# One 8 KB tile in place of two 4 KB ones for streamed expert weights, and router logits on four column tiles, in a two-layer decoder trunk

## The chip, the cores and the metric

The kernel runs on one core of a Trainium2 chip. The metric is the device time of one execution in microseconds (us). The engines are named as in the profile: PE is TensorE (PEld its weight loads), DVE is VectorE, ACT is ScalarE, POOL is GpSimd, SP is SyncE, whose queue issues nearly all DMAs here. A "tile" of weights below is 128 partitions x 2048 f32, which is 1 MB (1,048,576 bytes).

## The reference

256 tokens of 1024 channels go through two layers. Layer 0 is a mixer (attention beside a recurrent block) and a dense SwiGLU. Layer 1 is a pooling mixer and a mixture of 8 experts, two for each token. Cut to layer 1, which the change mostly touches:

```python
def rms_norm(x, g, eps=NORM_EPS):
    xf = x.astype(jnp.float32)
    y = xf * lax.rsqrt(jnp.mean(xf * xf, axis=-1, keepdims=True) + eps)
    return (y * g.astype(jnp.float32)).astype(x.dtype)
...
def pool_mixer(h, pool_w, pool_scale):
...
    for g, w in enumerate(POOL_WINDOWS):          # 4 groups of channels, windows 2, 4, 8, 16
...
        outs.append((cs - lower) / count - xg)    # mean over the window, minus the token itself
    d = jnp.stack(outs, axis=2).astype(h.dtype)
    y = jnp.einsum("bsgc,gcd->bsgd", d, pool_w).reshape(bsz, seq, D_MODEL)
    return y * pool_scale
...
def moe_swiglu(h, router_w, wg, wu, wd):
    t = h.reshape(-1, dm)
    logits = (t @ router_w).astype(jnp.float32)           # 256 x 8
    top_val, top_idx = lax.top_k(logits, TOP_K)           # 2 of 8
    gates = jax.nn.softmax(top_val, axis=-1)
    combine = jnp.sum(jax.nn.one_hot(top_idx, N_EXPERTS) * gates[..., None], axis=1)
    for e in range(N_EXPERTS):
        he = jax.nn.silu(t @ wg[e]) * (t @ wu[e])         # 1024 -> 3584
        out = out + (combine[:, e:e + 1] * he) @ wd[e]    # 3584 -> 1024
...
            h = h + pool_mixer(rms_norm(h, ln_mix_odd[j]), pool_w[j], pool_scale[j])
            h = h + moe_swiglu(rms_norm(h, ln_ffn_odd[j]), router_w[j], moe_wg[j], moe_wu[j], moe_wd[j])
    return rms_norm(h, final_g)
```

## The kernel before

**Streams and slots.** All weights are listed once, in the order of use (`order`), as 1 MB tiles: layer 0, one for the pooling mixer, then the experts' (`m_gu`, `m_dn`: 8 experts x 7 steps x 6 tiles = 336). `load_to` takes the next tile of the list, takes the next slot of the list `slots`, and issues the DMA on SP's queue; a slot is an SBUF buffer that is used again when the tile in it has been used. SP is strictly in order, and the DMAs go through eight completion semaphores in turn (`DMAHW0` to `DMAHW7` in the waits below), so that a DMA is issued only after the one eight places before it has landed. `load_free` issues as many loads as there are free slots. The number of slots grows as the program frees memory: `more_slots` puts a buffer at the head of the list; by the experts' stage there are 22.

**Splits.** Up to the pooling mixer the weights are used as pairs of fp32r numbers: `split_half` takes half a tile, ACT writes its rounded part (`hi`) and DVE or POOL the rest (`lo`). Both come from the pool `halves`, tags `hi` and `lo`, five buffers of 4 KB a partition each. When the splits run out, these buffers become slots of the experts' stream: the class `Two` takes one `hi` and one `lo` buffer, and a 1 MB tile is loaded into them by two DMAs of 512 KB, whose rows are 4 KB a partition (`twohi`, `twolo`). There are five such slots among the 22; the other 17 are 8 KB a partition and take one DMA of 1 MB.

**From the dense layer to the experts** the work is one chain. The last `down` piece of the dense layer is added to `h`; PE transposes `h`; ACT and DVE write its halves `xph`, `xpl` (`halve_pair`, four pairs); `rs` (1/rms of each token) comes from the sums of squares `ssq` by nine small DVE steps (`rs_steps`); PE multiplies with the pooling weights (`pw`); ACT and DVE scale the result with `rs` and halve it (`hh`, `hl`); PE applies the windows (`pd`); DVE adds to `h`; PE transposes again and ACT and DVE copy to `hT`. Then the router: `logits` multiplies `hT` with `rw` (16 products with 8 columns, two PE instructions each), `finish_rs` makes the new `rs`, DVE ranks the logits (`ahead`, `rank`, `mskb`), PE counts positions (`pos`), and DVE writes the selection `selr`, which holds `rs`. PE gathers the first expert's tokens with it (`xe`). `keep_warm` issues bf16 products that nobody reads.

**The experts' stage** runs 56 steps. In each, `gate_up_main` multiplies the tokens with four tiles of `m_gu` (`mg`), `gate_up_more` does the same for tokens beyond 64 where an expert has them (`go`), and `down_main`, `down_more` use two tiles of `m_dn` (`y`, `yo`). A step's four `m_gu` slots are given back when its last `mg` product has been issued (`finished`).

## Time and profile before

| | |
|---|---|
| time, median of 3 runs | 1165.93 us (1165.09 to 1167.14) |
| the profiled execution's own time | 1164.08 us |
| its span in the profile | 1162.2 us |
| PE, DVE, ACT, POOL busy | 96%, 26%, 21%, 7% of the span |
| DMA engines' share, mean rate | 87.7%, 352 GB/s |
| read from HBM | 406.62 MB |

"Busy" is a mean over stages with different limits, and a busy PE is not PE at its peak. DMA share is how much of the time the 16 DMA engines moved packets; slightly over 1 means that packets overlap.

### The profile page before, as it was taken

The numbers are of one execution on the slowest core, as the hardware profiler recorded it, in microseconds if no ns is written. First come the engines' busy times: TensorE is split into PE (matmuls) and PEld (weight loads), VectorE is DVE, ScalarE is ACT, GpSimd is POOL, SyncE is SP. The second block draws the span as 40 slices with busy tenths as digits, with TensorE's granted clock in tenths as the row PEclk, the third lists the DMA queues.
The fourth block names the chain that finished last, engine by engine and source line by source line (L and its number), as shares of the span: only waits on it lengthen the run. The fifth ranks groups of instructions, "written<-read, shape, count | busy, mean of one in ns | idle before, by whom it ended". The sixth has DMA issues, their size and how long they took to land.

```text
span 1162.2 us, 16786 instructions
## 1 busy us (share of the span) xinstructions
PE 1116.7 (96%) x7033; PEld 575.3 (50%) x7033; DVE 303.2 (26%) x592; ACT 248.3 (21%) x499; POOL 87.1 (7%) x110
## 2 busy tenths in 40 slices
PE   8999999999999999988989999999999999999995
PEld 7777999999843333322323343333334433433331
DVE  6686565454721111110101110111110011011112
ACT  5865544444510010010001000100000010001012
POOL 1613151121200000000000000000000000000000
PEclk9999999999999999999999999999999999999998
DMA  9434955555999999999999999999999999999991
GB/s 357 159 136 174 364 195 184 186 178 183 331 366 417 418 415 419 416 417 419 414 421 413 420 414 417 418 400 421 415 418 406 417 419 415 420 387 420 415 414 64
DMA packets 69910, 409.19 MB, mean 352 GB/s; under 512 B 7856, under 2 KB 8112, under 8 KB 31536
## 3 DMA queue, kind: packets, MB, share of 16 engines
q1 hardware_dynamic: 69664, 407.60, 87.7%
q8 instruction: 80, 1.31, 0.5%
q10 hardware_dynamic: 144, 0.10, 0.0%
q14 instruction: 22, 0.18, 0.0%
HBM read 406.62 MB, written 1.05 MB: 351 GB/s over the span
## 4 chain that ended last, share of the span: by engine, by line
PE 69%; DMA 22%; DVE 4%; ACT 3%; issue 1%; SPq 0%; DVEq 0%; ACTq 0%
PE mg L970 24%; PE y L1016 11%; PE gu L185 11%; DMA raw<-in_m_gu 8%; PE go L981 6%; PE dn L185 5%; PE yo L1026 3%; DMA raw<-in_m_dn 3%; PE xe L952 2%; DMA spare<-in_m_gu 2%; PE tp L1005 2%; DMA spare<-in_m_dn 1%; DMA twolo<-in_m_gu 1%; DMA twohi<-in_m_gu 1%; DMA sparehl<-in_m_gu 1%; PE wo L185 1%
## 5 line engine op out<-in xcount | busy, mean ns | idle before, releaser
L970 PE MATMUL mg<-raw,xe 128*64 128x512 f32 x928 | 219.9, 601 | 11.6 <-DMA raw<-in_m_gu 11.3
L999 DVE TENSOR_TENSOR sg<-sg,mg 128x256 f32<-128x256 f32 x56 | 23.6, 421 | 581.9 <-ACT sg L998 581.9
L998 ACT ACTIVATE sg<-mg 128x256 f32<-128x256 f32 x56 | 21.5, 383 | 560.4 <-PE mg L970 560.4
L168 DVE TENSOR_TENSOR lo<-raw,hi 128x1024 fp32r<-128x1024 f32 x84 | 106.3, 1285 | 97.9 <-ACT hi L167 97.6
L970 PEld LDWEIGHTS mg<-raw,xe 128*64 128x64 f32 x928 | 59.4, 136 | 126.6 <-issue 92.6
L167 ACT ACTIVATE hi<-raw 128x1024 fp32r<-128x1024 f32 x96 | 98.7, 1051 | 43.6 <-PE dn L185 25.0
L1016 PE MATMUL y<-raw,het 128*64 128x512 f32 x432 | 99.3, 594 | 1.1 <-DMA raw<-in_m_dn 1.0
L1007 ACT COPY het<-tp 128x384 f32<-128x384 f32 x56 | 26.7, 477 | 169.3 <-PE tp L1005 169.3
L1016 PEld LDWEIGHTS y<-raw,het 128*64 128x64 f32 x432 | 30.6, 137 | 64.6 <-issue 56.4
L970 PE MATMUL mg<-twolo,xe 128*64 128x512 f32 x212 | 55.5, 602 | 0.6 <-DMA twolo<-in_m_gu 0.6
L970 PE MATMUL mg<-twohi,xe 128*64 128x512 f32 x212 | 55.3, 604 | 0.7 <-DMA twohi<-in_m_gu 0.7
L1016 PE MATMUL y<-twohi,het 128*64 128x512 f32 x120 | 54.8, 593 | 0.5 <-ACT het L1007 0.5
L1016 PE MATMUL y<-twolo,het 128*64 128x512 f32 x120 | 54.7, 593 | 0.2 <-DMA twolo<-in_m_dn 0.2
L185 PE MATMUL gu<-xfl,hi 128*128 128x256 f32 x352 | 50.3, 283 | 0.0
L185 PE MATMUL gu<-xfh,hi 128*128 128x256 f32 x352 | 50.1, 283 | 0.0
L185 PE MATMUL gu<-xfh,lo 128*128 128x256 f32 x352 | 50.1, 283 | 0.0
L185 PEld LDWEIGHTS gu<-xfh,hi 128*128 128x128 f32 x352 | 46.2, 191 | 0.9
L185 PEld LDWEIGHTS gu<-xfl,hi 128*128 128x128 f32 x352 | 45.7, 192 | 0.2 <-DVE xfl L270 0.2
L185 PEld LDWEIGHTS gu<-xfh,lo 128*128 128x128 f32 x352 | 45.7, 192 | 0.0
L970 PE MATMUL mg<-spare,xe 128*64 128x512 f32 x168 | 41.3, 602 | 3.1 <-DMA spare<-in_m_gu 3.1
L981 PE MATMUL go<-raw,xe 128*32 128x256 f32 x704 | 41.8, 380 | 0.0
L1005 PEld LDWEIGHTS tp<-pr,sg 128*128 128x128 f32 x168 | 17.4, 141 | 46.4 <-issue 44.6
(380 smaller groups left out, 1372.9 us busy)
## 6 DMA issues: line engine op xcount, KB each, us to landing
raw<-in_m_gu SPq DMA_DIRECT2D x116, 1024.0 KB, 18.6
raw<-in_m_dn SPq DMA_DIRECT2D x54, 1024.0 KB, 19.0
twohi<-in_m_gu SPq DMA_DIRECT2D x53, 512.0 KB, 13.8
twolo<-in_m_gu SPq DMA_DIRECT2D x53, 512.0 KB, 12.6
raw<-in_w_gu SPq DMA_DIRECT2D x22, 1024.0 KB, 5.0
spare<-in_m_gu SPq DMA_DIRECT2D x21, 1024.0 KB, 15.9
twohi<-in_m_dn SPq DMA_DIRECT2D x30, 512.0 KB, 13.8
...
```

Source lines behind the costliest of these rows:

```text
L167: act.activation(hi, r, AF.Copy)
L168: eng.tensor_tensor(lo, r, hi.bitcast(F32), op=OP.subtract)
L185: pe.matmul(dst, l, r, start=start, stop=stop)
L952: pe.matmul(v_[:, k], h[:, t, (4 * k4 + k) * P:(4 * k4 + k + 1) * P], s_[:, t, :], start=t == 0, stop=t == NT - 1)
L970: pe.matmul(b[c * C0:(c + 1) * C0], x_[:, k, 0:C0], block(MOE[n] + k // 2, (k % 2 * 2 + c) * 512), start=k == 0, stop=k == 1)
L981: pe.matmul(go[q:q + C1, 0:2 * P], x_[:, k, C0:CAP], block(MOE[n] + k // 2, (k % 2 * 2 + c) * 512 + r * 2 * P, 2 * P), start=k == 0, stop= ...
L998: act.activation(v_, g_[:, :, 0, :], AF.Silu)
L999: dve.tensor_tensor(v_, v_, g_[:, :, 1, :], op=OP.mult)
L1005: pe.transpose(b[:, i * P:(i + 1) * P], sg[:, i, :], ident)
L1007: act.copy(het[n].rearrange("p a c -> p (a c)"), b[:, 0:3 * P])
L1016: pe.matmul(y_[e][j * C0:(j + 1) * C0], het[n][:, r, c * C0:(c + 1) * C0], block(DOWN[n] + c, (2 * j + r) * 512), start=p == c == r == 0, ...
L1026: pe.matmul(yo[q:q + C1], het[n][:, 2, (2 * c + r) * C1:(2 * c + r + 1) * C1], block(DOWN[n] + c, (2 * j + r) * 512), start=p == r == 0, s ...
```

## The change

It does three things. (1) `hi` and `lo` of a half tile become the two halves of one tile (`hl`, tag `two`, 8 KB a partition, five buffers), so a slot made of one takes one DMA of 1 MB, like the others. (2) `rw` is padded with zeros from 8 to 32 columns, and the logits are made transposed: `rw` is the stationary side, four products with 256 moving columns run on four column tiles of PE, twice; DVE copies the four partial sums (`lp`), PE transposes them back, DVE adds them up in two reductions. (3) For the second `rs`, DVE does the first two steps and POOL the other ten; they stand ahead of the reductions in the program. Beside that, in the pooling mixer all four pairs are halved before the steps to the first `rs`, where these steps stood between the pairs; `selr` takes `rw`'s buffer; two `keep_warm` counts go from 8 to 12 and from 4 to 5. The load of `rw` now writes 8 pieces of 32 bytes a partition, and waits for POOL's memset of `rw`.

```diff
-WARM = (8, 4, 8)
+WARM = (12, 5, 8)
...
-    class Two:
-
-        def __init__(self):
-            self.t = [halves.tile([P, W // 2], F32, tag=t_, name="two" + t_) for t_ in ("hi", "lo")]
...
+    def two():
+
+        return Again(halves.tile([P, W], F32, tag="two", name="two"))
...
-            cut = 2 if i < 2 or isinstance(r, list) else 4 if i == len(order) - 1 else 1
+            cut = 2 if i < 2 else 4 if i == len(order) - 1 else 1
...
-                sp.dma_start(r[a] if isinstance(r, list) else r[:, s_], order[i][1][:, s_])
+                sp.dma_start(r[:, s_], order[i][1][:, s_])
...
-        hi, lo = split[i, a] = [halves.tile([P, W // 2], F32R, tag=tag, name=f"{tag}{i}{a}") for tag in ("hi", "lo")]
+        both = halves.tile([P, W], F32R, tag="two", name=f"hl{i}{a}")
+        hi, lo = split[i, a] = [both[:, u * W // 2:(u + 1) * W // 2] for u in range(2)]
...
+    def finish_rs_pool(part):
+        v_, t_, w_ = nwt[:, 0, 0:NT], nwt[:, 1, 0:NT], nwt[:, 1, 4:4 + NT]
+        if part == 0:
+            dve.scalar_tensor_tensor(v_, ssq[:, :, 0], 1e-6, ssq[:, :, 1], op0=OP.add, op1=OP.add)
+            dve.tensor_scalar(rs.bitcast(I32), v_.bitcast(I32), -0.5, float(0x5F1FFFF9), op0=OP.mult, op1=OP.add)
+            return
+        pool.tensor_tensor(t_, rs, rs, op=OP.mult)
...
+        pool.tensor_tensor(rs, rs, t_, op=OP.mult)
...
-    rw = late.tile([P, KD, E], F32, name="rw")
+    rw = late.tile([P, KD, C1], F32, name="rw")
...
-        sp.dma_start(rw, rtr)
+        pool.memset(rw, 0.0)
+        sp.dma_start(rw[:, :, 0:E], rtr)
...
-    more_slots([Two(), Two()])
+    more_slots([two(), two()])
...
+    for kk in range(2, 4):
+        halve_pair(kk, tb[kk], xp, lno)
     squares(1, (1,))
-    halve_pair(2, tb[2], xp, lno, steps)
-    for step in steps:
-        step()
+    finish_rs()
...
-    run_piece(pool_products, {0: [F(halve_pair, 3, tb[3], xp, lno)], 1.5: [F(mixed_out, 0, 0)],
+    run_piece(pool_products, {1.5: [F(mixed_out, 0, 0)],
...
-    def logits(b):
-        for t in range(NT):
-            for k in range(KD):
-                pe.matmul(b[:, t * E:(t + 1) * E], hT[:, k, t * P:(t + 1) * P], rw[:, k, :], start=k == 0, stop=k == KD - 1)
+    def logits():
+
+        b = bank("tp", "lg")
+        for k2 in range(2):
+            for q in range(4):
+                pe.matmul(b[q * C1:(q + 1) * C1, 0:S], rw[:, 4 * k2 + q, :], hT[:, 4 * k2 + q, :], start=k2 == 0, stop=k2 == 1)
+        squares(1)
+        lp = keep.tile([P, S], F32, tag="row", name="lp")
+        dve.tensor_copy(lp, b[:, 0:S])
+        b = bank("gu", "lt")
+        for t in range(NT):
+            pe.transpose(b[:, t * P:(t + 1) * P], lp[:, t * P:(t + 1) * P], ident)
+        keep_warm(WARM[0], ones)
+        finish_rs_pool(0)
+        for t in range(NT):
+            dve.tensor_reduce(lg[:, t], b[:, t * P:(t + 1) * P].rearrange("p (q e) -> p e q", q=4)[:, 0:E, :], axis=AX.X, op=OP.add)
...
-    squares(1)
-    finish_rs()
-    lgb = bank("tp", "lg")
-    logits(lgb)
+    logits()
+    finish_rs_pool(1)
...
-    keep_warm(WARM[0], ones)
-
-    dve.tensor_copy(lg, lgb[:, 0:NT * E].rearrange("p (t e) -> p t e", t=NT))
```

Where instructions move, in the order of the program. SP's queue before, at the point where the slots of the splits join the experts' stream (`raw`, `spare` are slots of one 1 MB tile; `DMAHW` numbers are the eight completion semaphores):

```order
L144 DMA raw_3051<-in_m_dn 128x2048 [waits DMAHW4_49,DVE_49]
L144 DMA twohi<-in_m_gu 128x1024 [waits DMAHW5_49,PE_49]
L144 DMA twolo<-in_m_gu 128x1024 [waits DMAHW6_49,PE_49]
L144 DMA raw_3100<-in_m_gu 128x2048 [waits DMAHW7_49,DVE_49]
L144 DMA twohi<-in_m_gu 128x1024 [waits DMAHW0_49,PE_49]
L144 DMA twolo<-in_m_gu 128x1024 [waits DMAHW1_49,PE_49]
L144 DMA twohi<-in_m_gu 128x1024 [waits DMAHW2_49,PE_49]
L144 DMA twolo<-in_m_gu 128x1024 [waits DMAHW3_49,PE_49]
L144 DMA twohi<-in_m_dn 128x1024 [waits DMAHW4_49,PE_49]
L144 DMA twolo<-in_m_dn 128x1024 [waits DMAHW5_49]
```

The same place of the changed kernel:

```order
L140 DMA raw_2958<-in_m_dn 128x2048 [waits DMAHW4_49,DVE_49]
L140 DMA two<-in_m_gu 128x2048 [waits DMAHW5_49,PE_49]
L140 DMA raw_3003<-in_m_gu 128x2048 [waits DMAHW6_49,DVE_49]
L140 DMA two<-in_m_gu 128x2048 [waits DMAHW7_49,PE_49]
L140 DMA two<-in_m_gu 128x2048 [waits DMAHW0_49,PE_49]
L140 DMA two<-in_m_dn 128x2048 [waits DMAHW1_49,PE_49]
```

Each pair of 512 KB DMAs is one of 1 MB; which tile goes to which slot stays the same. PE before, from the last transposes of `h` to the first `keep_warm`:

```order
L258 MATMUL xt_3327<-pr,h 128x128 x3
L836 MATMUL lg<-rw,hT 128x8 [waits DMAHW2_49]
L836 MATMUL lg<-rw,hT 128x8
L836 MATMUL lg<-rw,hT 128x8 [waits DVE_49]
L836 MATMUL lg<-rw,hT 128x8
L836 MATMUL lg<-rw,hT 128x8 [waits Activation_49]
L836 MATMUL lg<-rw,hT 128x8
L836 MATMUL lg<-rw,hT 128x8 [waits DVE_49]
L836 MATMUL lg<-rw,hT 128x8 x9
L89 LDWEIGHTS cs
```

and in the changed kernel:

```order
L272 MATMUL xt_3222<-pr,h 128x128 x3
L852 MATMUL lg<-hT,rw 32x256 [waits DMAHW2_49]
L852 MATMUL lg<-hT,rw 32x256
L852 MATMUL lg<-hT,rw 32x256 [waits DVE_49]
L852 MATMUL lg<-hT,rw 32x256
L852 MATMUL lg<-hT,rw 32x256 [waits Activation_49]
L852 MATMUL lg<-hT,rw 32x256
L852 MATMUL lg<-hT,rw 32x256 [waits DVE_49]
L852 MATMUL lg<-hT,rw 32x256
L858 MATMUL lt<-pr,lp 128x128 [waits DVE_49]
L858 MATMUL lt<-pr,lp 128x128
L89 LDWEIGHTS cs
```

Sixteen products became eight, and a pair of transposes that waits for DVE's copy stands behind them. DVE of the changed kernel from the last copy to `hT` to the selection (`rt__1111` holds the logits, then the ranks):

```order
L882 COPY hT<-xt_3222 128x512 [waits PE_49]
L855 COPY lp<-lg 128x256 [waits PE_49]
L249 SCALAR_TENSOR_TENSOR nwt<-ssq 128x2 [waits Activation_49]
L250 TENSOR_SCALAR rs<-nwt 128x2 [waits DVE_49]
L862 TENSOR_REDUCE rt__1111<-lt 128x8 [waits PE_49]
L862 TENSOR_REDUCE rt__1111<-lt 128x8
L889 TENSOR_TENSOR ahead<-rt__1111 128x16x8 [waits DVE_49]
...
L959 TENSOR_SCALAR selr<-cs,rt__1111,rs 128x96 [waits DVE_49,Pool_49]
```

and POOL of the changed kernel, which before has nothing between the scaling of the pooling weights and the end:

```order
L252 TENSOR_TENSOR nwt<-rs 128x2 [waits DVE_49]
L253 TENSOR_TENSOR nwt<-nwt 128x2 [waits Pool_49]
L254 TENSOR_SCALAR nwt<-nwt 128x2 [waits Pool_49]
...
L260 TENSOR_SCALAR nwt<-nwt 128x2 [waits Pool_49]
L261 TENSOR_TENSOR rs<-rs,nwt 128x2 [waits Pool_49]
```

Of the nine `rs` steps that DVE had ahead of the copy of the logits, two are left there; the other ten are a chain on POOL, each waiting for the one before, and `selr` now waits for POOL too.

## Rows read from the trace of the kernel before

**Rows 1.** Busy time by stretch of the span (us from its start): length, then busy us and instructions of PE, PEld, DVE, ACT, POOL; granted clock of PE; DMA share; GB/s.

```profile
337.00:480.00 143.00, 142.17 (x691) 51.72 (x693) 19.31 (x50) 13.45 (x38) 0.00 (x0) 1.00 1.01 414
480.00:608.70 128.70, 112.71 (x506) 34.88 (x502) 13.55 (x34) 10.43 (x29) 0.00 (x0) 1.00 1.02 418
608.70:784.00 175.30, 175.30 (x1225) 66.14 (x1227) 21.54 (x53) 14.19 (x39) 0.00 (x0) 1.00 1.01 414
784.00:822.00 38.00, 33.37 (x161) 11.12 (x155) 3.08 (x7) 2.54 (x7) 0.00 (x0) 1.00 1.01 419
822.00:1143.00 321.00, 320.91 (x2298) 120.48 (x2298) 35.33 (x86) 24.73 (x69) 0.00 (x0) 1.00 0.99 403
```

**Rows 2.** The chain of work that ended last, in order of time: start, length, what.

```profile
588.75 19.88 DMA raw<-in_m_gu
...
802.05 19.88 DMA raw<-in_m_gu
...
821.98 1.94 PE mg L970 x8
```

**Rows 3.** SP's queue, issues in order of time: start, length, engine, line, what.

```profile
322.84 0.33 SPq L144 DMA_DIRECT2D spare<-in_m_dn  x1
335.91 2.57 SPq L144 DMA_DIRECT2D raw<-in_m_gu  x4
```

**Rows 4.** Stretches of 2 us, columns as in rows 1.

```profile
324.00:326.00 2.00, 1.94 (x14) 1.13 (x12) 1.22 (x7) 0.46 (x2) 0.00 (x0) 0.50 1.00 418
...
334.00:336.00 2.00, 2.00 (x13) 0.60 (x11) 0.00 (x0) 0.00 (x0) 0.00 (x0) 1.00 0.21 82
336.00:338.00 2.00, 1.06 (x6) 0.18 (x4) 0.62 (x2) 0.55 (x2) 0.00 (x0) 1.00 0.56 115
```

**Rows 5.** Stretches in which nearly all bytes moved in 4 KB packets (`twohi`, `twolo`), columns as in rows 1.

```profile
370.20:377.20 7.00, 7.00 (x41) 3.43 (x39) 0.56 (x1) 0.48 (x1) 0.00 (x0) 1.00 1.02 409
420.40:427.40 7.00, 7.00 (x35) 2.46 (x34) 2.04 (x3) 1.05 (x2) 0.00 (x0) 1.00 1.03 410
...
522.00:527.40 5.40, 4.99 (x24) 1.66 (x24) 0.87 (x2) 0.48 (x1) 0.00 (x0) 1.00 1.02 406
```

**Rows 6.** Stretches in which all data moved in 8 KB packets (the other slots).

```profile
381.00:412.00 31.00, 31.00 (x155) 11.61 (x153) 3.70 (x9) 3.09 (x9) 0.00 (x0) 1.00 1.01 420
...
533.00:562.00 29.00, 24.48 (x112) 8.08 (x114) 3.30 (x11) 2.06 (x6) 0.00 (x0) 1.00 1.01 421
```

**Rows 7.** DMA packets of 337 to 822 us, and below of 337 to 609 us.

```profile
DMA packets 34243, 201.48 MB, mean 415 GB/s; under 512 B 3793, under 2 KB 3793, under 8 KB 15583
...
DMA packets 19098, 113.12 MB, mean 416 GB/s; under 512 B 2112, under 2 KB 2112, under 8 KB 8512
```

**Rows 8.** DVE in order of time: start, length, line, what, shapes, count, and in brackets the idle time ahead of it and what ended that. Where a count is over 1, the length is that of all together.

```profile
309.10 0.48 DVE L270 SCALAR_TENSOR_TENSOR xpl<-xt,pr,xph 128x256 fp32r<-128x256 f32 x1 [0.41 <-ACT xph L268]
...
311.41 0.88 DVE L270 SCALAR_TENSOR_TENSOR xpl<-xt,pr,xph 128x256 fp32r<-128x256 f32 x2
312.30 2.07 DVE L216 SCALAR_TENSOR_TENSOR hl<-pw,rs,hh 128x512 fp32r<-128x512 f32 x3
...
319.33 0.69 DVE L856 COPY hT<-xt 128x512 f32<-128x512 f32 x1 [0.21 <-PE xt L258]
320.88 0.16 DVE L243 SCALAR_TENSOR_TENSOR nwt<-ssq 128x2 f32<-128x2 f32 x1 [0.86 <-ACT junk L239]
321.07 0.17 DVE L223 TENSOR_SCALAR rs<-nwt 128x2 int32<-128x2 int32 x1
...
323.01 0.29 DVE L867 TENSOR_TENSOR ahead<-rt__1143 128x128 bf16<-128x128 f32 x1
...
324.87 0.57 DVE L937 TENSOR_SCALAR selr<-cs,rt__1143,rs 128x96 f32<-128x96 f32 x2
```

**Rows 9.** PE in order of time, columns as in rows 8.

```profile
311.36 0.40 PE L185 MATMUL pw<-lo,xph 128*128 128x256 f32 x2
311.95 0.78 PE L185 MATMUL pw<-hi,xpl 128*128 128x256 f32 x2 [0.20 <-DVE xpl L270]
...
314.00 0.28 PE L817 MATMUL pd<-hh,ba 128*128 128x256 f32 x1
...
319.13 3.64 PE L836 MATMUL lg<-rw,hT 128*128 128x8 f32 x32
...
325.56 4.06 PE L952 MATMUL xe<-selr,h 128*128 128x96 f32 x32
```

**Rows 10.** Pieces of PE in the chain that ended last: products on four column tiles (32 products, 64 instructions), and a later gather.

```profile
660.30 3.59 PE go L981 x64
...
671.54 1.96 PE xe L952 x16
```

**Rows 11.** POOL in order of time, early in the kernel, where it does a chain of operations on 4 columns.

```profile
37.84 1.03 POOL L357 TENSOR_TENSOR st<-st 128x4 f32<-128x4 f32 x1
38.95 0.22 POOL L356 TENSOR_SCALAR st<-st 128x4 f32<-128x4 f32 x1
39.26 0.20 POOL L357 TENSOR_TENSOR st<-st 128x4 f32<-128x4 f32 x1
39.54 0.22 POOL L356 TENSOR_SCALAR st<-st 128x4 f32<-128x4 f32 x1
```

**Rows 12.** DVE at the time of the first of rows 11.

```profile
37.59 1.22 DVE L168 TENSOR_TENSOR lo<-raw,hi 128x1024 fp32r<-128x1024 f32 x1
```

More of the change, by code (lines that the diff above doesn't have):

```diff
@@ L110, in hybrid_kernel @@
     slots = [(raws, None)] * RA
-    class Two:
-        def __init__(self):
-            self.t = [halves.tile([P, W // 2], F32, tag=t_, name="two" + t_) for t_ in ("hi", "lo")]
-        def tile(self, *a, **k):
-            return self.t
     class Again:
@@ L247, in finish_rs @@
             step()
+    def finish_rs_pool(part):
[5 more added lines that the diff above has]
+        pool.tensor_tensor(t_, rs, rs, op=OP.mult)
+        pool.tensor_tensor(t_, t_, v_, op=OP.mult)
+        pool.tensor_scalar(t_, t_, -0.703952253, 0.703952253 * 2.38924456, op0=OP.mult, op1=OP.add)
+        pool.tensor_tensor(rs, rs, t_, op=OP.mult)
+        pool.tensor_tensor(t_, rs, rs, op=OP.mult)
+        pool.tensor_tensor(t_, t_, v_, op=OP.mult)
+        pool.tensor_scalar(w_, t_, 0.375, -1.25, op0=OP.mult, op1=OP.add)
+        pool.tensor_tensor(t_, t_, w_, op=OP.mult)
+        pool.tensor_scalar(t_, t_, 1.875, None, op0=OP.add)
+        pool.tensor_tensor(rs, rs, t_, op=OP.mult)
     def new_xt(name):
@@ L694, in bands @@
         for k in range(KD):
-            pool.tensor_scalar(rw[:, k, :], rw[:, k, :], pr[:, Q_LNR + k:Q_LNR + k + 1], None, op0=OP.mult)
+            pool.tensor_scalar(rw[:, k, 0:E], rw[:, k, 0:E], pr[:, Q_LNR + k:Q_LNR + k + 1], None, op0=OP.mult)
         i8 = iota[:, 0:E]
@@ L772, in hybrid_kernel @@
     lno = pr[:, Q_LNO:Q_LNO + 8]
-    steps = rs_steps()
-    more_slots([Two()])
+    more_slots([two()])
     run_piece(down(FC - 1), {1.5: [F(add_half, 0, 0)], 2: [F(squares, 0, (0,))], 2.5: [F(add_half, 0, 1)],
                              3: [F(squares, 0, (1,)), F(add_half, 1, 0), F(squares, 1, (0,))]}, (0,), pool)
-    more_slots([Two(), Two()])
+    more_slots([two(), two()])
     load_free()
@@ L821, in band_out @@
         dve.tensor_add(hv, hv, pd[t, n])
-    run_piece(pool_products, {0: [F(halve_pair, 3, tb[3], xp, lno)], 1.5: [F(mixed_out, 0, 0)],
+    run_piece(pool_products, {1.5: [F(mixed_out, 0, 0)],
                               2.5: [F(mixed_out, 1, 0)], 3.5: [F(mixed_out, 0, 1)]}, eng=pool)
-    more_slots([Two(), Two()])
+    more_slots([two(), two()])
     load_free()
@@ L911, in hybrid_kernel @@
     xe, het, y_ = {}, {}, {}
-    selr = late.tile([P, NT, P], F32, name="selr")
+    selr = late.tile([P, NT, P], F32, tag="rw", name="selr")
     late_room = {}
@@ L962, in block @@
     def block(i, j, n=512):
-        r = raw[i]
-        return r[j // 1024][:, j % 1024:j % 1024 + n] if isinstance(r, list) else r[:, j:j + n]
+        return raw[i][:, j:j + n]
     def gate_up_main(n, b, k):
```

## The prediction

> **What bounds the kernel now.** I began with the busy times by stretch [rows 1]. From 337 us on the DMA engines never rest: their share is 1.01 or more up to 822. PE, nominally 96% busy, rests 16.0 us of the 128.7 between 480 and 608.7, and 4.6 us of the 38 between 784 and 822; between these, and after 822, it does not rest. The chain of waits says the same [rows 2]: PE's work at 608.7 and at 822 starts as a tile lands (588.75 + 19.88, 802.05 + 19.88), and from 822 on the chain is PE's alone. So the end is set by (a) when the DMA stream starts to run without a break, (b) how long it takes for what lands before 822, (c) PE's work after that. The change leaves (c) alone.
>
> For (a) I read SP's queue [rows 3]. After 322.84 nothing is issued until 335.91, since all slots are full; the issue then is the first step giving its four tiles back. Meanwhile the DMA engines run dry: shares of 0.21 and 0.56 in two stretches of 2 us [rows 4] are 1.58 + 0.88 = 2.46 us without work. A first step that begins x us earlier moves the stream by x, up to about that 2.46 us.
>
> For (b) I compared stretches of one packet size. In 4 KB packets the rate is 409, 410 and 406 GB/s [rows 5], mean 408.3, which is 2.568 us a tile; in 8 KB packets 420 and 421 [rows 6], mean 420.5, 2.494 us. A tile in a two-part slot thus costs the stream 0.074 us more than another, while the DMA share is as high in both.
>
> **The stream.** Between 337 and 822 there were 15583 - 3793 = 11790 packets of 4 KB, or 46.05 tiles, and 8512 - 2112 = 6400, or 25.0 tiles, up to 609 [rows 7]. All of them become 8 KB packets of a form that the other slots already use, so I price them like those: 46 x 0.074 = **3.4 us**. Bounds from the extremes of the two groups: 410 against 420 gives 2.8, 406 against 421 gives 4.2; nothing at all if the two sets of stretches differ for another reason than the packets. At 608.7 the gain would be 25 x 0.074 = 1.9; PE then reaches 784 only that much earlier, but rests 4.6 us before 822, so the further 1.5 come out of that rest and the whole 3.4 counts at 822.
>
> The Trainium skill weighs against this: "DMA: Bandwidth & Descriptors", section Specifications, puts the minimum transfer for line rate at 512 B, by which 4 KB and 8 KB would run alike and this term would be nothing. The rows differ by 3% here, and I go by them.
>
> **The stage ahead of the experts.** Four steps.
>
> Pooling products. DVE now does all four pairs of `xpl` before the steps to `rs`. The two that came last (0.88 us) move ahead of them, and the 0.41 us that DVE waited for ACT go, since ACT's sum of squares no longer stands between the pairs [rows 8]: `rs` and `hl` are 0.47 late. PE gains: it started the third pair of instructions at 311.95 where 0.12 a product asks for 311.60, and spent about 0.3 more inside it [rows 9], so it could reach `pd` at 313.35 in place of 314.00. The first `hl`, done about 313.05 before (the first 0.75 of the three from 312.30), is done at 313.5 now. `pd` starts at 313.55, **0.45 earlier**; bounds nothing and 0.65.
>
> Logits. Before, 32 instructions take 3.64 us from 319.13, and the ranking starts at 323.01. Now the last four products wait for the last `hT`, 319.33 + 0.69 = 320.02. On four column tiles 64 instructions, eight such groups, took 3.59 us [rows 10], so 0.45 a group: 320.5. The copy `lp` has half the columns of the one at 319.33, 0.35 to 0.45: 320.95. Two transposes, at 0.12 each plus the passage through PE, about 0.4, two reductions of 0.2: ranking from about 321.95, 1.05 earlier, and 1.5 with the step above.
>
> The second `rs`. DVE's two steps come right behind `lp` (the sums of squares were there at 320.88 [rows 8]): 320.97 to 321.35. Then ten dependent operations on POOL. The nearest rows are those on four columns: starts 0.31 and 0.28 apart, undisturbed; 1.03 for one that ran beside a DVE subtraction of 1.22 us [rows 11, 12]. DVE's operations during the ranking are of the kind of the 0.29 us one, so I take 0.33 a piece: 3.3 us, `rs` at 324.7, with the 0.45 above 324.25. Without that wait `selr` could start at 324.87 - 1.5 = 323.4. So the logits' gain goes mostly into the wait for POOL, and `selr` starts 0.6 earlier, not 1.5. The bounds: 1.5 earlier if POOL were as quick as need be; 1.1 later at 0.5 a piece.
>
> "GPSIMD Engine Reference", section Engine selection, of the Trainium skill advises against this move too: elementwise work with two inputs is about twice as slow there as on VectorE. On operations this small the rows show 0.28 to 0.31 against DVE's 0.19 from start to start (320.88, 321.07), so 1.5 to 1.6 times.
>
> The gather. `xe` takes 4.06 us for 32 instructions, at a granted clock that was 0.50 until about 326 (the lower level, 1.2 GHz) after the 8-column products [rows 4, 9]; later 16 take 1.96 [rows 10], which makes 3.92. The denser products and twelve bf16 ones instead of eight may keep the clock up: 0.15.
>
> Sum of the stage: 0.6 + 0.15 = **0.75 us earlier**, bounds 1.65 earlier and 1.1 later. It lies inside the 2.46 us of dry DMA engines, so it moves the stream in full.
>
> **Edits at nothing.** The padded `rw` is loaded early in the dense layer and read by PE only at its end; its 1024 small pieces, and the wait for POOL's memset, delay tiles for which ten slots read ahead. The trace has no such load; were it as long as a whole tile, 2.5 us, and that cover gone, the dense layer would be 2.5 us later. A split's ACT half now waits for the buffer's `lo` readers too; the halves are made two pieces ahead of their use. If a split were late, PE would wait at `gu` or `dn` in the dense layer, and each such wait would count in full.
>
> **Sum.** 3.4 + 0.75 = 4.15 us. The profiled execution took 1164.08 us (span 1162.2, 1.9 around it): 1159.9. That execution was 1.85 below the median of 1165.93 and below all three timed runs, so against the median I forecast 1165.93 - 4.15 = **1161.8 us**. Its own range, with the bounds above: 2.8 - 1.1 = 1.7 to 4.2 + 1.65 = 5.85 less, 1160.1 to 1164.2.
>
> **Rivals.**
>
> The packet size doesn't matter. The stream's rate is then as before, and only the stage's 0.75 remains: 1165.2. For it: the rule above; the DMA share is over 1 in both groups; the 4 KB stretches are short (5 to 7 us). Against it: three of three are below both 8 KB ones by more than these differ among themselves. Chance 0.14.
>
> The tile as a whole. A tile in a two-part slot could be used when its first half had landed; now it must land whole, half of 2.49, 1.25 us later. That costs only where PE waits last, at 822. The tiles that end the waits at 608.7 and 822 lie in `raw` slots, whose rule doesn't change, and the assignment of slots stays; but a shift of some us may let the last wait fall on a neighbour: 1161.8 + 1.25 = 1163.05. Chance 0.10.
>
> `rs` on POOL makes it slower. `selr` waits for it, and everything behind `selr`: the gather, the first step, the first slots given back. If each of the ten operations took what the slow one in rows 11 took, 1.03 plus 0.09 of gap, the chain would be 11.2 us, 7.9 more than I took, and the result 3.75 later than before, 1169.7. It outweighs the stream from 0.75 us a piece on, and is slower by 0.2% from about 1.0. For it: POOL is slowed by DVE's work beside it, and DVE is at work there. Against it: the slow row stood beside a DVE operation of 1.22 us, and there is none of that size. Chance 0.04.
>
> **How the numbers follow.** Forecast 0.72, the rivals 0.14, 0.10, 0.04. About 0.2% (2.3 us) is what a measurement of this kernel can tell from no change. Of the forecast 0.67 lies beyond that and 0.05 within; of the second rival 0.08 and 0.02; the first is within, with 0.01 slower; the third is 0.03 slower, 0.01 within. Faster 0.75, same 0.21, slower 0.04. The range reaches from 1159.0 (a little more than my own bounds, for the run to run spread of 1 us) to 1165.0, which leaves out most of the first rival and the third.
>
> **What would show it.** Right: no DMA of 512 KB in the experts' stage; a rate of about 420 GB/s from 340 to 820; PE's rest of 16 us before 608 down by about 2, that before 822 still above 2; the first issue after the full slots at about 335.2; `selr` waiting for POOL. Wrong: stretches of `two` tiles at 408; POOL operations over 0.5; a wait for a `two` tile as the last before PE's unbroken stretch; a DMA gap after 322 that grows.

## The result, and the profile after

The median fell from 1166.12 us (1165.09 to 1167.14, five runs) to **1159.55 us** (1159.31 to 1160.21, five runs), a ratio of 0.9944 (95% interval 0.9932 to 0.9956). The forecast was 1161.8 within 1159.0 to 1165.0. The profiled execution took 1159.55 us (span 1157.7). Against the profiled execution of before, 2 us below its own median, the span fell by only 4.5; where the rest is turns out to be the main thing to learn here.

The changed kernel by stretch, columns as in [rows 1]:

```profile
337.00:480.00 143.00, 143.00 (x696) 51.77 (x694) 19.32 (x50) 13.26 (x38) 0.00 (x0) 1.00 1.01 419
480.00:605.50 125.50, 109.30 (x498) 34.09 (x494) 12.94 (x32) 9.87 (x27) 0.00 (x0) 1.00 1.01 420
605.50:782.00 176.50, 176.50 (x1231) 66.50 (x1233) 21.55 (x53) 14.19 (x39) 0.00 (x0) 1.00 1.01 420
782.00:822.00 40.00, 37.61 (x214) 13.56 (x214) 3.09 (x7) 2.54 (x7) 0.00 (x0) 0.96 1.01 421
822.00:1138.00 316.00, 316.00 (x2240) 118.29 (x2232) 35.35 (x86) 24.62 (x68) 0.00 (x0) 1.00 0.97 401
```

The picture is that of before: PE waits for tiles until about 605 and once more until 812, and then runs to the end. The rate, 414 to 419 before [rows 1], is 419 to 421 up to 822. The chain that ended last has the two landings, as in [rows 2], and the issue of a `two` tile is now one DMA (line, queue, KB, us to landing):

```profile
584.99 20.46 DMA raw<-in_m_gu
...
791.81 20.37 DMA raw<-in_m_gu
```

```profile
two<-in_m_gu SPq DMA_DIRECT2D x53, 1024.0 KB, 19.9
```

SP's queue around the full slots, the answer to [rows 3], and PE, DVE and POOL in the stage ahead of the experts, the answer to [rows 8, 9] (start, length, line, what):

```profile
320.03 0.33 SPq L140 DMA_DIRECT2D spare<-in_m_dn  x1
334.24 2.35 SPq L140 DMA_DIRECT2D raw<-in_m_gu  x4
```

```profile
306.84 0.72 PE L182 MATMUL pw<-hl,xph 128*128 128x256 f32 x4
...
313.15 0.39 PE L831 MATMUL pd<-hh,ba 128*128 128x256 f32 x1
...
318.46 1.48 PE L852 MATMUL lg<-hT,rw 128*32 128x256 f32 x16
320.47 0.44 PE L858 MATMUL lt<-pr,lp 128*128 128x128 f32 x2 [0.53 <-DVE lp L855]
...
324.16 3.78 PE L974 MATMUL xe<-selr,h 128*128 128x96 f32 x32 [0.71 <-DVE selr L959]
```

```profile
321.27 0.29 DVE L889 TENSOR_TENSOR ahead<-rt__1111 128x128 bf16<-128x128 f32 x1
...
323.69 0.57 DVE L959 TENSOR_SCALAR selr<-cs,rt__1111,rs 128x96 f32<-128x96 f32 x2 [0.52 <-POOL rs L261]
```

```profile
320.77 0.19 POOL L252 TENSOR_TENSOR nwt<-rs 128x2 f32<-128x2 f32 x1 [20.72 <-DVE rs L250]
...
323.46 0.19 POOL L261 TENSOR_TENSOR rs<-rs,nwt 128x2 f32<-128x2 f32 x1
```

`pw` starts at 306.84 where it started at 307.20 before. So 0.36 us of every gain that is read from the start of the span lies ahead of the stage; below, times in the stage are counted from `pw`. The first issue after the full slots comes 1.67 earlier, which is 1.31 counted from `pw`, and not 0.75.

**One ruler for all traces.** Four marks can be read in each trace from PE in order of time: the first `pw`, the first transposes of the experts' first step (`tp`), those of its 36th step (the first whole step after the wait at 812 or 822), the end of the span. Between them lie the stage, the stream and PE's unbroken work. The `tp` rows of the kernel before, and then of the changed one:

```profile
337.83 0.55 PE L1005 MATMUL tp<-pr,sg 128*128 128x128 f32 x3 [0.94 <-DVE sg L999]
...
831.88 0.55 PE L1005 MATMUL tp<-pr,sg 128*128 128x128 f32 x3
```

```profile
336.16 0.55 PE L1026 MATMUL tp<-pr,sg 128*128 128x128 f32 x3 [0.94 <-DVE sg L1020]
...
827.21 0.55 PE L1026 MATMUL tp<-pr,sg 128*128 128x128 f32 x3
```

All times of the table are in us.

| trace | first `pw` | stage | stream | rest to the end | span |
|---|---|---|---|---|---|
| before | 307.20 | 30.63 | 494.05 | 330.3 | 1162.2 |
| before, again | 306.73 | 33.85 | 493.73 | 330.3 | 1164.7 |
| after | 306.84 | 29.32 | 491.05 | 330.5 | 1157.7 |
| after, again | 307.31 | 29.33 | 490.67 | 330.5 | 1157.8 |
| only the 8 KB tiles (t1) | 306.91 | 33.12 | 490.60 | 330.4 | 1161.0 |
| after with 8-column logits (u1) | 307.29 | 30.76 | 490.60 | 330.5 | 1159.2 |
| after with 8 and 4 warming products (t2) | 307.15 | 29.38 | 491.26 | 330.5 | 1158.3 |
| after with 1/rms on DVE (t3) | 307.15 | 29.79 | 490.97 | 330.5 | 1158.4 |
| after, `two` by 4 KB rows (s1) | 308.08 | 29.37 | 493.30 | 330.2 | 1160.9 |
| after, all by 4 KB rows (s3) | 307.97 | 29.32 | 505.33 | 331.3 | 1173.9 |
| after, 4 KB pieces in one DMA (s5) | 307.25 | 29.31 | 503.56 | 330.5 | 1170.6 |
| after, `two` by even and odd (s6) | 307.20 | 29.33 | 490.33 | 330.2 | 1157.1 |
| after with one more slot (c1) | 307.31 | 29.31 | 489.09 | 330.5 | 1156.2 |

### The profile page after: what moved, and what is told of

It reads as the page before. It is cut to its first block, busy times and chain, and to the rows that moved or that the text cites. A ratio compares the mean times of both kernels' runs of the same rounds, so it can differ in the third digit from the quotient of the medians.

```text
span 1157.7 us, 16595 instructions
## 1 busy us (share of the span) xinstructions
PE 1112.1 (96%) x7024; PEld 571.7 (49%) x7024; DVE 303.3 (26%) x587; ACT 249.8 (22%) x499; POOL 89.7 (8%) x121
## 3 DMA queue, kind: packets, MB, share of 16 engines
q8 instruction: 80, 1.31, 0.5%
## 4 chain that ended last, share of the span: by engine, by line
PE 55%; DMA 16%; DVE 0%; ACT 0%; issue 0%; DVEq 0%; ACTq 0%; SPq 0%
PE mg L991 27%; PE y L1037 13%; DMA raw<-in_m_gu 7%; PE go L1002 6%; DMA raw<-in_m_dn 4%; DMA spareh<-in_m_gu 3%; PE yo L1047 3%; PE xe L974 2%; PE tp L1026 2%; DMA two<-in_m_gu 2%; PE sc L1076 1%; PE st L1062 0%; PE go L1009 0%; ACT junk L236 0%; DVE yt L213 0%
## 5 line engine op out<-in xcount | busy, mean ns | idle before, releaser
L165 DVE TENSOR_TENSOR hl<-raw,hl 128x1024 fp32r<-128x1024 f32 x84 | 107.6, 1289 | 96.8 <-ACT hl L164 95.6
L164 ACT ACTIVATE hl<-raw 128x1024 fp32r<-128x1024 f32 x96 | 100.5, 1055 | 44.6 <-PE dn L182 17.5
L991 PE MATMUL mg<-two,xe 128*64 128x512 f32 x424 | 102.1, 602 | 2.5 <-DMA two<-in_m_gu 2.5
L182 PE MATMUL gu<-xfh,hl 128*128 128x256 f32 x704 | 94.3, 283 | 0.0
L182 PEld LDWEIGHTS gu<-xfh,hl 128*128 128x128 f32 x704 | 89.3, 192 | 0.9
L182 PE MATMUL dn<-hl,heth 128*128 128x512 f32 x176 | 57.0, 396 | 0.0
L1037 PE MATMUL y<-two,het 128*64 128x512 f32 x240 | 54.8, 593 | 0.7 <-ACT het L1028 0.5
L182 PE MATMUL gu<-xfl,hl 128*128 128x256 f32 x352 | 50.3, 283 | 0.0
L182 PEld LDWEIGHTS gu<-xfl,hl 128*128 128x128 f32 x352 | 45.7, 192 | 0.2 <-DVE xfl L284 0.2
L182 PE MATMUL dn<-hl,hetl 128*128 128x512 f32 x88 | 34.9, 396 | 0.0
```

The source lines that it names most:

```text
L164: act.activation(hi, r, AF.Copy)
L165: eng.tensor_tensor(lo, r, hi.bitcast(F32), op=OP.subtract)
L182: pe.matmul(dst, l, r, start=start, stop=stop)
L991: pe.matmul(b[c * C0:(c + 1) * C0], x_[:, k, 0:C0], block(MOE[n] + k // 2, (k % 2 * 2 + c) * 512), start=k == 0, stop=k == 1)
L1037: pe.matmul(y_[e][j * C0:(j + 1) * C0], het[n][:, r, c * C0:(c + 1) * C0], block(DOWN[n] + c, (2 * j + r) * 512), start=p == c == r == 0, ...
```

## Experiments

**1. The kernel before, again.** No edit.

> The kernel before once more, unchanged, for a second trace of it beside the others on the same chip. The medians fell by 6.57 us (1166.12 to 1159.55), the profiled spans by 4.5 (1162.2 to 1157.7). Theory (the first profiled execution of the kernel before was 2 us quicker than its median somewhere that the change does not touch, by the clock early in the program or after 822): this span is 1163 to 1165, and set against it step by step the changed kernel gains 1.3 to 1.7 in the stage and 3.4 to 3.7 in the stream, with the rest ahead of 300 us or behind 822. Rival (the changed kernel really gains 6.6 and the trace of it misses some of that): the steps from 337 to 822 of this trace are later than those of the first by 2 us.

Median 1166.18 against 1165.56 of the kernel before's other runs in the same session (ratio 1.0004, 0.9994 to 1.0013): the same kernel. In this trace the stage takes 33.85 us, 3.2 more than in the first. The granted clock by stretch, and PE's two rows there:

```profile
318.00:322.00 4.00, 4.00 (x36) 3.98 (x35) 2.66 (x11) 2.03 (x6) 0.00 (x0) 0.92 1.02 390
322.00:326.00 4.00, 3.94 (x23) 2.76 (x24) 2.49 (x12) 0.21 (x1) 0.00 (x0) 0.50 1.00 422
326.00:330.00 4.00, 4.00 (x20) 4.00 (x20) 0.42 (x1) 0.69 (x2) 0.00 (x0) 0.50 1.00 424
330.00:334.00 4.00, 4.00 (x22) 2.83 (x23) 1.45 (x7) 0.11 (x1) 0.00 (x0) 0.80 0.88 371
```

```profile
318.65 4.36 PE L836 MATMUL lg<-rw,hT 128*128 128x8 f32 x32
325.81 6.56 PE L952 MATMUL xe<-selr,h 128*128 128x96 f32 x32
```

The clock was at the lower level (0.50, 1.2 GHz) for (0.08 + 0.50 + 0.50 + 0.20) x 4 / 0.50 = 10.2 us here. In the first trace it was 3.4 us, from 322.7 on: (0.33 + 0.50 + 0.02) x 2 / 0.50, with [rows 4] and these two stretches of it:

```profile
322.00:324.00 2.00, 2.00 (x14) 1.63 (x15) 1.63 (x9) 0.00 (x0) 0.00 (x0) 0.67 1.02 422
...
326.00:328.00 2.00, 2.00 (x19) 2.00 (x19) 0.14 (x1) 0.44 (x1) 0.00 (x0) 0.98 1.03 434
```

In the second trace the logits cost 0.72 more (4.36 against 3.64) and the gather 2.5 more (6.56 against 4.06) [rows 9]. So the kernel before differs from itself by 3 us in this stage, and the first trace happened to be a cheap one. The theory was right in its first half (a span of 1163 to 1165) and wrong in where: neither ahead of 300 nor behind 822. The rival's sign is what is seen: the first step's `tp` is 2.75 us later, at 340.58. But it is the first trace of the kernel before that hides a part of the gain, and not the changed kernel's.

**2. Only the 8 KB tiles.** The kernel before with this part of the change alone (the slots change in the same way at two more places):

```diff
+    def two():
+
+        return Again(halves.tile([P, W], F32, tag="two", name="two"))
...
-            cut = 2 if i < 2 or isinstance(r, list) else 4 if i == len(order) - 1 else 1
+            cut = 2 if i < 2 else 4 if i == len(order) - 1 else 1
...
+        both = halves.tile([P, W], F32R, tag="two", name=f"hl{i}{a}")
...
-    more_slots([Two()])
+    more_slots([two()])
...
```

> The kernel before, with the 8 KB tiles for the two parts as the only change; pooling order, logits, 1/rms and the counts of warming products stay as before. Theory (stream 2.9 to 3.7, and the rest of the gain is the stage, of which part is a fall of the clock that the logits of 8 columns bring): 1161.9 to 1162.7 against 1165.6, with the granted clock at 0.50 for 3.4 us or a multiple from 321 on, as in both traces of the kernel before. Rival (the tiles are all of it): 1159.6. Rival (a split that waits for both halves of its buffer costs in the dense layer): over 1163, with waits of PE at `gu` or `dn`.

Median 1163.55 (1160.51 to 1164.42, twelve runs) against 1165.74, ratio 0.9977 (0.9966 to 0.9988): 2.2 us by the medians, 1.4 to 4.0 by the interval. That is 0.85 above the top of what was expected. In the trace the stream takes 490.60, as after the whole change, and the stage 33.12, with the clock down again:

```profile
322.00:326.00 4.00, 3.24 (x26) 2.39 (x25) 2.64 (x13) 0.78 (x2) 0.00 (x0) 0.78 1.01 428
326.00:330.00 4.00, 4.00 (x20) 4.00 (x20) 0.56 (x1) 0.13 (x1) 0.00 (x0) 0.50 1.01 422
330.00:334.00 4.00, 4.00 (x24) 2.48 (x25) 1.71 (x9) 0.20 (x1) 0.00 (x0) 0.87 0.73 303
```

That is (0.22 + 0.50 + 0.13) x 4 / 0.50 = 6.8 us at the lower level, from 324.2 on; here PE had rested 0.70 between the logits and the fall. In this trace the tiles give the stream's gain and nothing else; no wait of PE at `gu` or `dn` appears. The twelve executions fall in two groups: three took 1160.51 to 1161.06 at a granted clock of 0.991 to 0.993 (mean over the span), nine took 1162.86 to 1164.42 at 0.985 to 0.990. The trace is of the second group.

**3. `two` tiles by two DMAs of 4 KB rows.** The changed kernel, in which the slots made by `two()` carry `cut = 2`:

```diff
+        s_.cut = 2
...
+            own = getattr(r, "cut", 1)
...
-            cut = 2 if i < 2 else 4 if i == len(order) - 1 else 1
+            cut = 2 if i < 2 else 4 if i == len(order) - 1 else own
```

> The changed kernel, with one thing put back: a tile in a `two` slot is loaded by two DMAs of 512 KB, each of 4 KB rows, into the two halves of the same 8 KB tile. Theory (the row size sets the rate, 2.568 us a tile of 4 KB rows against 2.494): the waits that end at 605.5 and 812.2 end later by 25 x 0.074 = 1.9 and by 3.4 (up to 3.7, what the step-by-step comparison of the two traces shows between 336 and 809), the median goes from 1159.6 to 1163.0 to 1163.3, and the first issue after the full slots stays at 334.2. Rival (the row size does not matter, the stage ahead of the experts gave everything): 1159.6, within 0.5.

Median 1162.34 (ratio to before 0.9973, 0.9964 to 0.9983), 2.8 more than the changed kernel; the stream is 2.5 us longer than the mean of 490.8 of the seven traces (after, after again, t1, u1, t2, t3, s6) that have full-rate tiles in all slots. The theory holds in sign and mechanism; the median is 0.7 under the lower end of what was expected. This run also prices the rest of the change: with the row size of before, and a stream that is only 0.6 shorter than before (493.30 against 493.9), it is still 3.2 us below the kernel before (1165.56).

**4. All tiles by two DMAs of 4 KB rows**, `else 2 if i >= MOE0 else 1` in the same line.

> The changed kernel, with every tile of the experts loaded by two DMAs of 512 KB with 4 KB rows. Theory (row size): the rate is 408 GB/s from 340 on; some 190 tiles land between 337 and 812, 190 x 0.074 = 14.1 us, so at least 1173.6; since PE then waits for tiles beyond 812 as well, where it has been the slower of the two, up to 1181. Rival (the row size does not matter, or the 408 of the kernel before came from a mixture of two sizes): 1159.6 to 1162.

Median 1174.91, ratio to before 1.0076 (1.0058 to 1.0093). The median lies in what was expected (1173.6 to 1181), and the stream is 14.5 longer, against 14.1 expected:

```profile
480.00:600.00 120.00, 109.84 (x454) 32.73 (x450) 12.93 (x32) 9.08 (x26) 0.00 (x0) 1.00 1.03 408
600.00:780.00 180.00, 177.67 (x1219) 64.99 (x1218) 20.99 (x52) 14.19 (x39) 0.00 (x0) 1.00 1.02 408
```

**5. 4 KB pieces in one DMA of 1 MB.** The weights lie in memory with the two halves of a row 512 KB apart:

```diff
...
+                        sp.dma_start(r.rearrange("p (a w) -> p a w", a=2), order[i][1].rearrange("a p w -> p a w"))
...
+    m_gu, m_dn = (m.reshape(-1, P, 2, W // 2).transpose(0, 2, 1, 3) for m in (m_gu, m_dn))
```

> The changed kernel, with the experts' weights laid out in memory so that the two halves of each 8 KB row of a tile are 512 KB apart: every tile is still one DMA of 1 MB into one tile, over all partitions, but of 4 KB pieces. It tells the row size from the size and number of the DMAs. Theory (row size): the rate is 408 GB/s from 340 on and the median is that of the variant in which all tiles came by two DMAs of 4 KB rows, 1174.9 within 1.5. Rival (the number and size of the DMAs): 421 GB/s and 1159.6 to 1160.6.

Median 1172.8, ratio to before 1.0062 (1.0047 to 1.0076), stream 12.8 longer; 2.1 below the expected 1174.9 and so 0.6 outside its tolerance, but 12 from the rival's upper end:

```profile
480.00:600.00 120.00, 101.31 (x461) 31.52 (x459) 12.32 (x30) 8.84 (x24) 0.00 (x0) 1.00 1.03 409
600.00:780.00 180.00, 176.80 (x1229) 65.91 (x1225) 21.00 (x52) 14.66 (x40) 0.00 (x0) 1.00 1.03 409
```

One DMA a tile, as many issues and completions as after the change, and yet 409. So the length of the contiguous piece sets the rate, whether the two pieces of a row lie 4 KB apart (experiment 4) or 512 KB (here); twice as many DMAs add at most the last 2 us.

**6. Two DMAs of 512 KB with 8 KB rows**, first by partitions 0 to 63 and 64 to 127, then by even and odd partitions:

```diff
...
+                    p_ = slice(a * P // 2, (a + 1) * P // 2)
+                    sp.dma_start(r[p_], order[i][1][p_])
...
+                    even = lambda v_: v_.rearrange("(p a) w -> a p w", a=2)[a]
+                    sp.dma_start(even(r), even(order[i][1]))
```

> The changed kernel, with a tile in a `two` slot loaded by two DMAs of 512 KB that divide the partitions (0 to 63, 64 to 127) and keep rows of 8 KB. It tells the row size from the size and number of the DMAs. Theory (row size): as the changed kernel, 1159.6 within 0.7, and from the first step of the experts to the step that follows 812 no more than 0.5 us beyond what the changed kernel takes. Rival (what costs is the smaller DMA, one more issue and one more completion a tile): 1162.3, and 2.9 us more between those steps, as the variant with 4 KB rows had.

> The changed kernel, with a tile in a `two` slot loaded by two DMAs of 512 KB, the first for the even partitions and the second for the odd ones, both of 8 KB rows. The variant by partitions 0 to 63 and 64 to 127 moved 208 to 230 GB/s through such stretches, with all DMA engines busy. Theory (half of the partitions side by side are what halves the rate there, not the 64 rows of a DMA): the even and odd halves run at 418 to 421 GB/s and the median is 1159.7 within 1.0; this is then also the size of a DMA told apart from the size of a row. Rival (64 rows in a DMA are enough to halve it): stretches of 208 to 230 again and over 1400.

By halves side by side (partitions 0 to 63 and 64 to 127) the executions lay between 1422 and 1482 us: neither theory nor rival foresaw it. Here is one stretch of other tiles and one of such halves in that trace:

```profile
420.00:431.00 11.00, 9.01 (x40) 2.64 (x42) 2.04 (x3) 1.05 (x2) 0.00 (x0) 1.00 1.01 419
432.00:448.00 16.00, 9.35 (x33) 2.56 (x31) 0.62 (x2) 1.03 (x3) 0.00 (x0) 0.75 1.02 216
```

So the first variant could not tell what it was made for. The second could: by even and odd partitions the median is 1159.37, the stream 490.33, the rate

```profile
480.00:600.00 120.00, 105.57 (x482) 33.84 (x478) 12.93 (x32) 9.91 (x27) 0.00 (x0) 1.00 1.01 420
```

For these five slots, halving the DMA costs nothing as long as the rows stay at 8 KB and the halves are not side by side.

**7. The logits of before in the changed kernel** (32 products of 8 columns, no column tiles, transposes or reductions):

```diff
...
-                pe.matmul(b[q * C1:(q + 1) * C1, 0:S], rw[:, 4 * k2 + q, :], hT[:, 4 * k2 + q, :], start=k2 == 0, stop=k2 == 1)
+                pe.matmul(b[:, t * E:(t + 1) * E], hT[:, k, t * P:(t + 1) * P], rw[:, k, 0:E], start=k == 0, stop=k == KD - 1)
...
```

> The changed kernel with the logits of before: 32 products of 8 columns that write the sums at once, no column tiles, no transposes, no reductions; 12 and 5 warming products, pooling order and 1/rms on GpSimd stay. Theory (the 8-column products make the clock fall, whatever stands behind them): the granted clock is 0.50 for 3.4 us or a multiple from 321 to 324 on; from the first product of the pooling to the first transposes of the experts it takes 29.9 to 33.1 us in place of 29.3, and the median is 1160.6 to 1163.2. Rival (the warming products or the shorter wait for the gather keep it up): the clock stays at 1.00, the ranking starts 1.0 later, `selr` 0.5 later since the wait for GpSimd goes, 1160.1 within 0.4.

Median 1160.93 (1160.70 to 1164.44), 1.2 above the 1159.72 of the changed kernel in the same session. The clock falls again, for (0.40 + 0.02) x 4 / 0.50 = 3.4 us, though twelve warming products follow:

```profile
318.00:322.00 4.00, 4.00 (x39) 3.97 (x37) 1.72 (x4) 2.21 (x6) 0.72 (x4) 1.00 1.01 422
322.00:326.00 4.00, 3.94 (x28) 2.73 (x27) 2.41 (x11) 0.11 (x1) 1.37 (x7) 0.60 1.01 428
326.00:330.00 4.00, 4.00 (x34) 3.87 (x36) 0.68 (x2) 0.79 (x2) 0.00 (x0) 0.98 1.01 422
```

`selr` starts at 325.08, 17.79 behind `pw` instead of 16.85, so 0.94 later (the rival's price was 0.5, its clock wrong). Five of the six executions took 1160.70 to 1161.39 at a mean granted clock of 0.991, the sixth 1164.44 at 0.988.

**8. Fewer warming products**, `WARM = (8, 4, 8)` as before.

> The changed kernel with 8 and 4 warming products ahead of the gather instead of 12 and 5. Theory (the 8-column logits made the clock fall, 3.4 us in one trace of the kernel before and 10.2 in the other; the dense ones do not): the granted clock stays at 1.00 from 318 to 330, the gather takes 3.5 to 3.8 us, 1159.6 within 0.5. Rival (the added warming products hold it): the clock falls to 0.50 between 320 and 330 as before, the gather takes 4.1 us or more, and the stage ends 0.3 to 2.7 later, 1159.9 to 1162.3.

Median 1159.97, ratio to before 0.9952 (0.9935 to 0.9968). The clock stays up and the gather takes 3.78:

```profile
318.00:322.00 4.00, 3.47 (x34) 2.17 (x34) 2.74 (x9) 2.08 (x6) 0.68 (x3) 1.00 1.01 422
322.00:326.00 4.00, 2.30 (x23) 1.91 (x22) 1.81 (x9) 0.91 (x2) 1.50 (x7) 1.00 1.01 428
```

```profile
324.53 3.78 PE L974 MATMUL xe<-selr,h 128*128 128x96 f32 x32 [0.87 <-DVE selr L959]
```

With experiment 7 this settles whether the clock falls: it is the form of the logits, not the warming products behind them. All four traces with 8-column logits have the fall (3.4, 10.2, 6.8, 3.4 us), and none of the ten with dense ones. The share of busy time alone would have misled: PE is busy for all of 318 to 322 ahead of the fall, and in this trace only for 2.30 of the next 4 us, at full clock. How long the fall lasts is not settled: executions with a long one are the rule in t1 (nine of twelve, 8 and 4 warming products) and rare in u1 (one of six, 12 and 5), but these two differ in more than the warming products.

The run to run spread fits: 4.2 us over the kernel before's runs of all sessions (1163.34 to 1167.59), 3.9 and 3.7 in t1 and u1; 0.9 and 0.7 in the two sets of the changed kernel, 2.1 at most in the variants with dense logits and the stream as changed. But the clock is not all of it: of 64 executions of the kernel before, the 19 with a mean granted clock of 0.989 or less took 1165.56 to 1167.59 (median 1166.6), the other 45 took 1163.34 to 1167.09 (median 1165.4).

**9. The second 1/rms on DVE**, `finish_rs()` ahead of the reductions in place of the two parts of `finish_rs_pool`.

> The changed kernel with the second 1/rms on VectorE: the nine steps of before stand ahead of the two reductions, and GpSimd has none of it. Seven more steps at 0.19 are 1.3 us in DVE's row ahead of the ranking; the 0.52 us that `selr` waited for GpSimd go. Theory (the move to GpSimd paid, by 0.8): `selr` starts 0.8 later than in the changed kernel, counted from the first product of the pooling, and the median is 1160.4 within 0.5. Rival (the wait for GpSimd is the bound and DVE has the room): `selr` starts up to 0.5 earlier, 1159.1.

Median 1160.40 as expected, ratio to before 0.9955 (0.9943 to 0.9968). The stage is 0.47 longer; `selr` starts 0.47 later, counted from `pw` (17.32 against 16.85), and waits for nothing:

```profile
322.22 0.16 DVE L227 SCALAR_TENSOR_TENSOR rs<-nwt,rs 128x2 f32<-128x2 f32 x1
322.29 0.28 DVE L862 TENSOR_REDUCE rt__1111<-lt 128x8 f32<-128x32 f32 x2
...
324.47 0.57 DVE L958 TENSOR_SCALAR selr<-cs,rt__1111,rs 128x96 f32<-128x96 f32 x2
```

The move to GpSimd pays, with half a us, although DVE waits 0.52 for it. The expected 0.8 took all seven steps as added time, but DVE had 0.26 of idle time of its own ahead of the reductions.

**10. The changed kernel, again.** No edit.

> The changed kernel once more, unchanged, for a second trace beside the others on the same chip. Theory (its fall of the clock at 812 belongs to that one execution, the stage's does not return): the clock is 1.00 from 318 to 330, from the first product of the pooling to the first transposes of the experts it takes 29.3 us, and what the steps from there to the one behind 812 take agrees with the first trace to 0.3; with or without a fall at 812, 1159.6 within 0.7. Rival (falls come at random in both kernels): a fall of 3.4 us or more in the stage, and 30 us or more there.

Median 1159.72, ratio to before 0.9947 (0.9933 to 0.9962); stage 29.33, no fall there. The first trace had one at 812, right behind PE's last wait; eight `mg` took 3.59 there, and 1.88 once it was over:

```profile
812.22 3.59 PE L991 MATMUL mg<-raw,xe 128*64 128x512 f32 x8 [1.41 <-DMA raw<-in_m_gu]
815.64 1.88 PE L991 MATMUL mg<-spare,xe 128*64 128x512 f32 x8
```

The second trace has none, and its stream is 0.38 shorter, 0.08 more than the tolerance. That fall comes and goes, then, but is small.

**11. One more slot.** The changed kernel with a slot that is used once; it lies where `selg` and the second `xe` are later; to make room, the small third of `sg` moves to `sm`.

```diff
...
+               + [work.tile([P, W], F32, tag="room", name="onceroom", bufs=1)])
...
+        room = work.tile([P, W], F32, tag="room", name="room", bufs=1)
+        late_room.update(selg=room[:, 0:512].rearrange("p (t a s) -> p t a s", t=NT, a=2))
+        xe.append(room[:, 1024:1024 + KD * CAP].rearrange("p (k s) -> p k s", k=KD))
...
+        sm = keep.tile([P, S], F32, tag="row", name="sm")[:, 0:P]
...
```

> The changed kernel with one more slot for a tile, used once: it lies where `selg` and the second `xe` are from the fifth step on, and the small third of `sg` moves to the tile of the router's partial sums to make room. In the changed kernel the DMA engines still run dry for 2.9 us (332.2 to 336) ahead of the first step's end. Theory (the start of the unbroken stream is what moves the end): a tile of 2.49 us more goes into that gap, the waits that end at 605.5 and 812.2 end 2.3 to 2.5 earlier, and the median is 1157.2 within 0.7. Rival (the gap is not on the path, for instance since PE is the bound behind 812 and the rest before it would shrink instead): 1159.6.

Median **1157.22** (1157.17 to 1158.07) as expected, ratio to before 0.9927 (0.9915 to 0.9940), 2.3 to 2.5 below the changed kernel: the fastest of all. The gap in the changed kernel's first trace, then its second trace behind the gap, then this run:

```profile
332.00:334.00 2.00, 2.00 (x10) 0.43 (x6) 0.00 (x0) 0.00 (x0) 0.00 (x0) 1.00 0.15 57
334.00:336.00 2.00, 1.22 (x7) 0.29 (x5) 0.32 (x1) 0.55 (x2) 0.00 (x0) 1.00 0.43 66
```

```profile
338.00:340.00 2.00, 2.00 (x12) 0.71 (x10) 0.00 (x0) 0.00 (x0) 0.00 (x0) 1.00 1.03 430
```

```profile
332.00:334.00 2.00, 2.00 (x12) 0.58 (x8) 0.00 (x0) 0.00 (x0) 0.00 (x0) 1.00 1.01 422
...
338.00:340.00 2.00, 2.00 (x12) 0.72 (x10) 0.00 (x0) 0.00 (x0) 0.00 (x0) 1.00 1.03 320
```

In the trace the stream is only 1.6 shorter than in the changed kernel's second one. About 0.5 is lost at 338 to 340, where the rate is 320 against 430, for a reason that stays open. And the profiled execution was the slowest of the five, 0.85 above their median, so its stream shows less than the medians do.

## Why the prediction came out as it did

The mechanism was right and the total too small: 4.15 us forecast, 6.57 measured (6.09 with the changed kernel's second set, 1165.81 to 1159.72). The result lies 2.25 under the forecast, and 0.55 under the lower end that the bounds of the terms gave (1160.1). It lies inside the stated range only because that range reached 1.1 us lower for the run to run spread, which is luck and no merit of the sum. Two terms were mis-sized, in opposite directions: the stream a little too large, the stage far too small. By experiment 3, all but the row size is worth about 3 us of the median, where the stage was put at 0.75.

- **The stream, 3.4.** Right in cause: rows of 4 KB move at 408, rows of 8 KB at 420, in three ways (experiments 3 to 5), and the DMA's own size is excluded (6). By the ruler it was worth 493.9 - 490.8 = 3.1, and 2.5 with experiment 3, whose medians say 2.8. So the term was a little large, at its lower bound or under it.
- **The Trainium skill**, "DMA: Bandwidth & Descriptors", section Specifications, with line rate from 512 B on, would have made that term nothing. The traces disagree: 3% between 4 and 8 KB.
- **Whether it counts in full.** Yes. PE still rests 2.39 us between 782 and 822, so the landing at 812 sets the rest, which is 330.2 to 330.5 us in all traces of the ruler but one, where tiles run late to the end.
- **Pooling order, 0.45.** `pd` starts 6.31 behind `pw`, before 6.80: 0.49.
- **Logits, 1.5 with that.** `ahead` starts 14.43 behind `pw`, before 15.81: 1.38.
- **GpSimd, 3.3 us for ten.** It took 2.88, from 320.77 to 323.65, 0.29 a piece. It was a little quicker than the 0.33 that was taken. So `selr` came 0.82 earlier (16.85 behind `pw` against 17.67) and not 0.6. The rival in which GpSimd makes the kernel slower is excluded by experiment 9.
- **The gather, 0.15.** This is the step that failed. I read the granted clock of 0.50 [rows 4], priced it by the one trace at 4.06 against 3.92, and took it for a constant. From `selr` to the first transposes of the experts the changed kernel takes 12.47, the first trace of before 12.96, so the gain there is 0.49. The second trace takes 15.46, 2.99 more than the changed kernel (2.78 of it in the gather, 6.56 against 3.78), and the fall costs 0.72 in the logits beside that; there the stage as a whole gains 4.53. So the clock's term is some 0.5 to 3.7, not 0.15. With 3.1 for the stream and 0.82 for `selr` that makes 4.4 to 7.6, which holds the 6.57; how the executions behind the median divide within it is not shown. A sign of it was in the numbers: the profiled execution lay below all three timed ones, and I moved the sum to the median without asking what differed.
- **The reference execution.** I made the sum against the profiled execution and moved it to the median. For terms that every execution shares that is right. Here the term that differs between executions was the very one that the change removes.
- **My own signs.** The first issue was to come at 335.2 (it came at 334.24), `selr` was to wait for POOL (0.52), no DMA of 512 KB in the experts' slots: right in kind. One sign of being wrong came as well: the DMA gap grew, from 2.46 us to (0.85 + 0.57) x 2 = 2.84 by the two stretches shown in experiment 11. What counts for the stream is the gap's end, and that came 1.67 earlier; the last issue ahead of the gap came earlier still (320.03 against 322.84). PE's rest before 608 was to fall from 16 to 14; it is 16.2. Between the same two steps the time did fall, from 105.86 (494.73 to 600.59) to 104.53 (493.06 to 597.59), but the profile books it as less busy time. Both signs were badly chosen; why the busy time is less is open.
- **The rivals.** "The packet size doesn't matter" is excluded by experiments 3 to 5. "The tile as a whole" was not seen: PE's last wait ends, as before, with a tile in a `raw` slot.

Open: why the fall lasts 3.4, 6.8 or 10.2 us, and how often each; what else spreads the kernel before's executions at a high clock; why `pw` starts up to 1.3 us earlier or later from one execution to the next (306.73 to 308.08), whatever the kernel; why the rate is 320 at 338 to 340 in experiment 11.
